# A third group of seven-product matrix forms in one gate stage, with one group's weight sums formed in SBUF

## The chip, the cores and the metric

The kernel runs on one core of one Trainium2 chip. The metric is the device time of one execution in microseconds (us); the time of a kernel is the median of its runs. Beside it one execution is profiled, and every duration below comes from that one. PE is the matrix engine (TensorE), DVE the vector engine, ACT the scalar engine, POOL is GpSimd, SP issues the plain loads.

## The reference, cut to what matters

Two layers work on 256 tokens of 1024 features in float32. Each layer is a feed-forward, a token mixer (causal pooling and attention, merged by gates) and a second feed-forward. Only the feed-forwards matter here:

```python
def swiglu(h, w_gate_up, w_down):
    a, b = jnp.split(h @ w_gate_up, 2, axis=-1)
    return (jax.nn.silu(a) * b) @ w_down

x = x + 0.5 * swiglu(rms_norm(x, ffn1_norm), ffn1_w_gate_up, ffn1_w_down)
...                                   # the token mixer
x = x + 0.5 * swiglu(rms_norm(x, ffn2_norm), ffn2_w_gate_up, ffn2_w_down)
```

`w_gate_up` has 2 x 2816 columns, 22 blocks of 128 for the gate and 22 for the other half. The results must stay float32-exact to a tight bound, so plain low-precision products are not enough.

## The kernel before, in words

**Units.** All weights lie in HBM as units of 128 x 2048 float32 (1 MB). A unit is loaded by SP into one of four `raw` buffers and split into two parts: ACT writes `hi`, the value rounded to the matrix engine's fast format (L209, two halves of 1024 columns), and DVE writes `lo` = raw - hi (L210). The activations are split in the same way. There are six half buffers each for hi and lo, so three units are split ahead of PE at most, and a split half waits until PE has read the half three units earlier.

**Pairs.** One unit of `w_gate_up` gives a gate block and its partner for all tokens: 16 products of a 512-column matmul (hi with both parts of x) and a 256-column one (lo with x's hi). The kernel calls that `pair`. The drained pair (ACT L258, DVE L259) is scaled, put through SiLU and multiplied in `post` (L465 to L474), and lands as two parts in a gate buffer: `ga`, `gb`, `gc` or `gd`.

**Groups and forms.** Four units can also be done as a group: x is cut into halves of its features and of its tokens, the weights likewise, and the 2 x 2 block product is made by seven products of sums of blocks instead of eight (Winograd's variant of Strassen). Each of the seven *forms* is half a unit's work for PE, but needs 1 MB of weights, loaded and split like a unit (L193 to L199). Forms 1, 2 and 3 read blocks of the weights as they lie; 4, 5, 6 and 7 read sums of blocks. Those sums are made long before, in DRAM: POOL copies one block to a DRAM tile and then lets the DMA add another (`go_on`, L183, one step a call, each behind the latest marked DVE result, L184). Form 6 starts from a copy of 7, form 4 from a copy of 6. `far_sums` lists the steps; the calls of `go_on` are spread over the whole kernel.

Products of a group accumulate in four PSUM banks, b0 to b3, each 128 x 512 (`banks4`). `seven` (L594) runs a form and combines its result: forms 1, 6 and 5 are copied out by ACT, forms 2, 5 and 4 are followed by a DVE addition that reads a bank (L607, L614, L619), and `gated` (L576 on ACT, L577 on DVE) multiplies SiLU of the gate half with its partner, for form 3 straight from the bank. The results have tokens on the partitions, so `turned` (t0, t1 of a group: four transposes each, L588) turns them through a bank, and ACT and DVE write the two parts from there to a gate buffer (L591, L592).

**Order.** PE's instructions keep the order of the program. The order of a gate stage is the tuple `TWO` or `THREE` (L54 to L57): a number is a pair, "7A" is form 7 of group A, "t1A" a turn, and (17, "t0B") a pair with a turn in its middle. The build orders the other engines' instructions itself; an engine takes them strictly in that order. The first feed-forward has no groups. The three others are called stage I (layer 0, second feed-forward, base `FU`, order TWO: 14 pairs, groups A and C), stage II (layer 1, first, base `LU`, order THREE: 10 pairs, groups A, B and C) and stage III (layer 1, second, THREE). In THREE, group B's products of forms 1, 6, 5, 3 go to b0 and those of A and C to b2; form 2 goes to b1, forms 7 and 4 to b3; t1 of A or B uses the bank of form 1, t0 uses b1, and C is turned during the down-projection that follows each gate stage.

Of the kernel before, what the change touches and what calls it, by code (L numbers as in the profile page):

```python
# [18 lines left out]
F32 = mybir.dt.float32  # L19
# [41 lines left out]
def groups_of(base):  # L61
    return "AC" if FEED[base] is TWO else "ABC"


def feed_units(base):

    for n in FEED[base]:
# [11 lines left out]
def trunk_kernel(ctx: ExitStack, tc: tile.TileContext, x_in, w_in, pw_in, qkn_in, rope_in, mask_in, band_in, out):  # L79
# [70 lines left out]
    far, steps_left = {}, []  # L150
# [9 lines left out]
    def far_sums():  # L160

        for base in STAGES:
            rest = []
            for g in groups_of(base):
# [21 lines left out]

    def sum_form(base, n):

        f, g = n
        z, hi, lo = buffers()  # L190
        src = quadrant(base, g, RAW[f]) if f in RAW else two_rows(far.pop((f, g, base)))
        z = two_rows(z)
        nc.sync.dma_start(z, src)  # L193
        z = z.rearrange("p i (k c) -> p i k c", c=2 * P)
# [5 lines left out]
        return hi, lo  # L200

    def buffers():
        raw = raws.tile([P, 2 * HALF], F32, name="raw", tag="raw")
        hi = [parts.tile([P, HALF], F32R, name="hi", tag="hi") for _ in range(2)]
        lo = [parts.tile([P, HALF], F32R, name="lo", tag="lo") for _ in range(2)]
        return raw, hi, lo
# [213 lines left out]
    def ffn(after, n0=0, end=False, col=None, base=0, far_at=(), steps_at=()):  # L420
        gs, gt = {}, {}

        def room(name, n0, m):
            g = acts.tile([P, m, 2, S], F32R, name=name, tag=name)
            gt[name] = g
            gs.update({n0 + i: g[:, i] for i in range(m)})

        def place(n):

            name, first = next(z for z in (("gb", 16), ("gd", 12), ("gc", 8), ("ga", 0)) if n >= z[1])  # L430
            return name, n - first

        room("ga", 0, 8)
        room("gc", 8, 4)
        room("gd", 12, 4)
        abs_, more = {}, []
        late_r = not (end and FEED[base] is TWO)
# [22 lines left out]
        def post(n):  # L460
# [10 lines left out]
            name, i = place(n)  # L471
            z = gt[name][:, i:i + 2]
# [4 lines left out]
        if n0:  # L477
            room("gb", 16, NF - 16)
# [17 lines left out]
        else:  # L496
# [12 lines left out]
            three = FEED[base] is THREE  # L509
            tk = {g: acts.tile([P, 2, GW], F32, name="tk", tag="tok", bufs=2) for g in ("AB" if three else "AC")}  # L510
            tk.setdefault("C", tk["A"])
# [13 lines left out]
            def x_forms():  # L525
# [26 lines left out]
                room("gb", 16, NF - 16)  # L552
# [27 lines left out]
            def turned(n, g):  # L580
# [3 lines left out]
                else:  # L584
                    pt = (bank["1" + g] if n == three else banks4[1]).rearrange("p (a s) -> p a s", s=S)
# [3 lines left out]
                name, i = place(GROUPS[g] + 2 * n)  # L589
                g = gt[name][:, i:i + 2]  # L590
# [3 lines left out]
            def seven(f, g):  # L594
# [3 lines left out]
                if f == "5":  # L598
                    if g == "B":
                        gated(p1, 0, 0, 0)  # L600
                    if three and g == "C":
                        p1 = tk["B"][:, 0]
                by_tokens(f, z, f in "127")
                if f == "1":
                    act(p1, z, AF.Copy)
                elif f == "2":
                    tt(p1, z, p1, op=OP.add)  # L607
                    if g != "B":
# [15 lines left out]
            if three:  # L624
                go_on()
# [532 lines left out]
```

## Time and profile before

| | |
|---|---|
| median of 3 runs | 994.12 us (994.01 to 995.92) |
| span of the profiled execution, first to last instruction | 991.9 us |
| PE busy | 986.1 us, 99% |
| DVE / ACT / POOL busy | 811.2 / 661.6 / 71.0 us |
| stage I, first gate matmul to first matmul of the down-projection | 325.38 to 439.74 |
| stage II | 499.37 to 612.01 |
| stage III | 815.18 to 927.82 |
| moved by DMA | 285.19 MB, mean 288 GB/s |
| loads of units and raw forms by SP (1 MB) | 168, median 7.2 us to landing |
| loads of sums by SP (1 MB) | 32, median 5.8 us to landing |
| steps in DRAM by POOL | 48 from the weights, 16 from another sum |

How to read the rows: a row of the groups has line, engine, operation, tiles (out<-in), shapes and count, then busy us and mean ns of one. A row of the timeline has start and duration in us, then the same names; "x2" marks two merged neighbours, and brackets hold the idle time before it and what ended it. Neighbours on DVE and ACT overlap a little. The ends of PE's matmuls are modelled, so the starts of its rows are what counts.

### The profile page before, as it was taken

Reading aid. Unit: us, or ns where it says so; the run is one execution under the profiler, and the core shown is the slowest. Engines: PE = TensorE matmul, PEld = TensorE weight load, DVE = VectorE, ACT = ScalarE, POOL = GpSimd, SP = SyncE. Lnnn points to the kernel's source line nnn. Section 1 sums busy time; section 2 is a strip of 40 time slices with the busy share of each in tenths; the row PEclk is TensorE's granted clock in tenths of the full one; section 3 lists DMA queues with packets and bytes.
Section 4 is the critical chain, followed back from the end, with each engine's and each line's share of the span. In section 5 each row is a group of like instructions: output and inputs, shape, how many; then the busy total and the mean of one; then the engine's idle time right before and its main releaser. Section 6 shows DMA issues by size and latency. Waiting matters only on the chain.

```text
span 991.9 us, 16162 instructions
## 1 busy us (share of the span) xinstructions
PE 986.1 (99%) x6296; PEld 895.4 (90%) x6296; DVE 811.2 (82%) x1154; ACT 661.6 (67%) x988; POOL 71.0 (7%) x111
## 2 busy tenths in 40 slices
PE   9999999999999999999999999999999999999998
PEld 8989888898899988889888889988988998888897
DVE  6987777698978798886779999776988887999872
ACT  7865555567766787775578877555677568887641
POOL 0000010104100000000000000000141000000000
PEclk9999999999999999999999999999999999999999
DMA  8889899989979769899979989898799998988840
GB/s 298 322 297 323 254 327 343 309 241 292 323 237 328 255 242 324 297 325 286 311 267 305 321 289 347 277 311 279 258 298 372 248 306 299 320 314 292 293 150 22
DMA packets 50269, 285.19 MB, mean 288 GB/s; under 512 B 4753, under 2 KB 6033, under 8 KB 27409
## 3 DMA queue, kind: packets, MB, share of 16 engines
q1 hardware_dynamic: 36624, 217.05, 58.8%
q0 software_dynamic: 13568, 67.11, 27.7%
q8 instruction: 49, 0.80, 0.3%
q14 instruction: 28, 0.22, 0.1%
HBM read 283.10 MB, written 68.16 MB: 354 GB/s over the span
## 4 chain that ended last, share of the span: by engine, by line
PE 99%; DMA 0%; DVE 0%; ACT 0%; SPq 0%; issue 0%
PE ps L110 68%; PE b L110 15%; PE pt L110 7%; PE two L110 4%; PE pe L110 1%; PE sc L110 1%; PE pt L780 1%; PE y L110 1%; PE b L588 0%; DMA raw<-w 0%; PE tp L736 0%; PE pt L588 0%; PE st L110 0%; PE ss L110 0%; DVE t L681 0%; ACT hi L209 0%
## 5 line engine op out<-in xcount | busy, mean ns | idle before, releaser
L210 DVE TENSOR_TENSOR lo<-raw,hi 128x1024 fp32r<-128x1024 f32 (+2 forms) x303 | 360.9, 1203 | 104.3 <-ACT hi L209 102.9
L209 ACT ACTIVATE hi<-raw 128x1024 fp32r<-128x1024 f32 (+2 forms) x303 | 310.6, 1033 | 194.8 <-PE ps L110 123.1
L110 PE MATMUL ps<-hx,hi 128*128 128x512 f32 x1184 | 400.2, 384 | 0.6 <-ACT hi L209 0.6
L110 PE MATMUL ps<-hx,lo 128*128 128x256 f32 x1184 | 323.7, 273 | 0.0
L110 PEld LDWEIGHTS ps<-hx,hi 128*128 128x128 f32 x1184 | 222.2, 188 | 40.7 <-ACT hi L209 0.8
L110 PEld LDWEIGHTS ps<-hx,lo 128*128 128x128 f32 x1184 | 222.5, 188 | 0.3 <-DVE lo L210 0.3
L199 DVE TENSOR_TENSOR lo<-raw,hi 128x1024 fp32r<-128x1024 f32 x112 | 135.0, 1220 | 17.7 <-ACT hi L198 17.5
L198 ACT ACTIVATE hi<-raw 128x1024 fp32r<-128x1024 f32 x112 | 117.5, 1056 | 41.4 <-PE ps L110 25.3
L110 PE MATMUL ps<-ga,hi 128*128 128x512 f32 (+1 forms) x264 | 87.8, 378 | 0.0
L110 PE MATMUL b<-hi,sf 128*128 128x512 f32 x256 | 87.4, 383 | 0.0
L183 POOL DMA_DIRECT2D f<-w x48 | 44.6, 932 | 557.7 <-DVE ab L259 239.4
L110 PE MATMUL b<-lo,sf 128*128 128x256 f32 x256 | 70.2, 274 | 0.0
L110 PE MATMUL ps<-ga,lo 128*128 128x256 f32 x256 | 69.9, 273 | 0.0
L110 PE MATMUL ps<-gb,hi 128*128 128x512 f32 (+1 forms) x198 | 65.4, 376 | 0.0
L110 PE MATMUL pt<-hi,hx 128*128 128x512 f32 x192 | 64.9, 384 | 0.0
L110 PE MATMUL b<-hi,hx 128*128 128x512 f32 x192 | 59.1, 388 | 0.0
L110 PEld LDWEIGHTS ps<-ga,hi 128*128 128x128 f32 x264 | 49.0, 188 | 8.2
L110 PEld LDWEIGHTS b<-hi,sf 128*128 128x128 f32 x256 | 48.0, 188 | 8.4
L110 PE MATMUL pt<-lo,hx 128*128 128x256 f32 x192 | 52.5, 274 | 0.0
L110 PE MATMUL ps<-gb,lo 128*128 128x256 f32 x192 | 52.4, 273 | 0.0
L110 PEld LDWEIGHTS ps<-ga,lo 128*128 128x128 f32 x256 | 48.1, 188 | 0.0
L110 PEld LDWEIGHTS b<-lo,sf 128*128 128x128 f32 x256 | 48.0, 188 | 0.0
(209 smaller groups left out, 1590.6 us busy)
## 6 DMA issues: line engine op xcount, KB each, us to landing
raw<-w SPq DMA_DIRECT2D x168, 1024.0 KB, 7.2
f<-w POOLq DMA_DIRECT2D x48, 1024.0 KB, 11.9
raw<-f SPq DMA_DIRECT2D x32, 1024.0 KB, 5.8
raw<-w SPq DMA_DIRECT2D x16, 256.0 KB, 5.3
out_dram<-gx SPq DMA_DIRECT2D x8, 128.0 KB, 1.9
gx<-x SPq DMA_DIRECT2D x3, 256.0 KB, 5.5
qk<-pw SPq DMA_DIRECT2D x2, 256.0 KB, 5.7
gx<-x SPq DMA_DIRECT2D x1, 300.0 KB, 2.8
```

The lines of the kernel that those rows point to most:

```text
L110: return keep(nc.tensor.matmul(*args, **kw))
L183: z = nc.gpsimd.dma_start(two_rows(far[f, g, base]), src, **kw)
L198: act(hv, a, AF.Copy)
L199: tt(lv, a, hv.bitcast(F32), op=OP.subtract)
L209: act(hi, w, AF.Copy)
L210: return tt(lo, w, hi.bitcast(F32), op=OP.subtract)
L780: keep(nc.tensor.transpose(pt[:, h, o * P:(o + 1) * P], pr[:, h, c * P:(c + 1) * P], ident))
```

## The change

- One order, `FEED`, with three groups now serves all three stages. Stage I so gets a group B: 10 pairs and 21 forms instead of 14 pairs and 14 forms. The forms stand in another order than in THREE, group C's spread over the stage.
- Group C's sums are no longer made in DRAM. `begin` loads a block by SP into a room in SBUF (the tiles of `gc` for 7, 6 and 4, of `gd` for 5), and POOL's DMA adds the second block there. Form 7C is split straight from the room; then POOL adds block 11 to the room for 6C, and after that split block 21 for 4C. The gate buffers `gc` and `gd` are allotted later for the results (`PLACES`), where the room is spent.
- The steps in DRAM fall from 64 to 48, with POOL's 12 additions into SBUF beside them; the calls of `go_on` are thinned.
- The banks: C has b0 (forms 1, 6, 5, 3) and b1 (7, 4); A and B have b2 (1, 6, 5, 3) and b3 (7, 4); form 2 of every group goes to b3. t1 of A or B turns through b2, t0 through b3.
- C's `gated(p1, 0, 0, 0)` moves from form 2 to form 3.

```diff
-TWO = (0, 1, "1A", 2, "2A", 3, 4, "7A", 5, "6A", 6, "5A", 7, "4A", "3A", 8, "t1A", "1C", (9, "t0A"), "2C", 10, "7C", 11, "6C",
-       16, "5C", 17, "4C", "3C")
-THREE = (0, 1, "1A", 2, "2A", "1B", 3, 4, "7A", "6A", 5, "5A", 6, "4A", "2B", "3A", "7B", "6B", 7, "t0A", "t1A", "5B",
-         16, "1C", "4B", "3B", "6C", (17, "t0B"), "7C", "t1B", "5C", "2C", "3C", "4C")
-FEED = {FU: TWO, LU: THREE, LU + FU: THREE}
+FEED = (0, 1, "+7C", "1A", "+5C", 2, "2A", "1C", 3, 4, "7A", "6A", 5, "5A", "7C", "4A", "3A", (6, "t1A"), "t0A", "1B", "2B", 7,
+        "6B", "7B", "5B", "6C", 16, "4B", "3B", "2C", "t1B", "5C", (17, "t0B"), "3C", "4C")
+PLACES = {"ga": range(8), "gb": (16, 17, 12, 13, 14, 15), "gd": range(8, 12), "gc": range(18, 22)}
+CHAIN = {"7": "11", "6": "21"}
...
+        while isinstance(u, tuple) and u[1][0] == "+":
+            begin(u[0], u[1][1:])
+            u = next(plan)
...
-            for g in groups_of(base):
+            for g in "AB":
...
+    def add_to(z, src):
+        nc.gpsimd.dma_start(two_rows(z), src, accum_op=OP.add)
+
+    def begin(base, n):
+        f, g = n
+        z = acts.tile([P, 2 * HALF], F32, name="c" + f, tag="gc" if f == "7" else "gd")
+        first, second = {"7": ("12", "22"), "5": ("11", "12")}[f]
+        nc.sync.dma_start(two_rows(z), quadrant(base, g, first))
+        add_to(z, quadrant(base, g, second))
+        near["5" if f == "5" else "764"] = z
+
     def sum_form(base, n):
         f, g = n
+        if g == "C" and f not in RAW:
+            hi, lo = halves_of_unit()
+            z = near["5" if f == "5" else "764"]
+            two_parts(z, hi, lo)
+            if f in CHAIN:
+                add_to(z, quadrant(base, g, CHAIN[f]))
+            return hi, lo
...
-            for g in groups_of(base):
-                for f in "1653":
-                    bank[f + g] = banks4[0 if (g == "B" if three else g == "A") else 2]
-                bank["2" + g] = banks4[1]
-                bank["7" + g] = banks4[3]
-                bank["4" + g] = banks4[3]
+            for g in GROUPS:
+                one, two = banks4[:2] if g == "C" else banks4[2:]
+                bank.update({f + g: one for f in "1653"})
+                bank.update({f + g: two for f in "74"})
+                bank["2" + g] = banks4[3]
...
-                    pt = (bank["1" + g] if n == three else banks4[1]).rearrange("p (a s) -> p a s", s=S)
+                    pt = bank["21"[n] + g].rearrange("p (a s) -> p a s", s=S)
...
-                name, i = place(GROUPS[g] + 2 * n)
-                g = gt[name][:, i:i + 2]
+                if GROUPS[g] not in gt:
+                    name = next(z for z in PLACES if GROUPS[g] in PLACES[z])
+                    room(name, PLACES[name])
+                g = gt[GROUPS[g] + 2 * n]
...
-            if l or h in (0, 2, 3, 4, 5, 7):
+            if h in (0, 2, 3, 4, 5, 7):
                 go_on()
...
-            far_at=(1,3,5,7,9) if l else (0,2,4,6,8,10), steps_at=(2,))
+            far_at=(1,3,5,7) if l else (0,2,4,6,8,10))
...
-            ffn(lambda f: prep(f, l + 1, C_G1), col=C_G2, base=FU, far_at=(1,3,5,7,9), steps_at=(3,6,10,16))
+            ffn(lambda f: prep(f, l + 1, C_G1), col=C_G2, base=FU, far_at=(1,5,9), steps_at=(3,))
```

How the new order moves instructions, at three places of stage II (stages I and III have the same order after the change). The line numbers of the changed kernel are its own.

First place: DVE, from the second lo half of the form ahead of 5A's addition. Before (`b3` is read by the additions of 5A, L614, and of 4A, L619; `vt` is what `gated` writes; `ab` belongs to the pairs):

```order
L199 TENSOR_TENSOR lo_5780<-raw_5776,hi_5778 128x2x2x256
L614 TENSOR_TENSOR tk_5313<-b3_5318,tk_5313 128x512
L465 TENSOR_TENSOR ab_5534<-ab_5534,r_5269 128x2x256
L199 TENSOR_TENSOR lo_5809<-raw_5806,hi_5807 128x2x2x256
L577 SCALAR_TENSOR_TENSOR vt_5312<-tk_5313,sg_5711 128x256
L470 TENSOR_TENSOR ab_5534<-ab_5534 128x2x256
L199 TENSOR_TENSOR lo_5810<-raw_5806,hi_5808 128x2x2x256
L259 TENSOR_TENSOR ab_5714<-ps_5715,ab_5714 128x512
L199 TENSOR_TENSOR lo_5836<-raw_5833,hi_5834 128x2x2x256
L619 TENSOR_TENSOR tk_5313<-b3_5318,tk_5313 128x512
```

And now (L634 and L639 are these additions, L595 is `gated`; the last row reads form 3A's bank b2):

```order
L221 TENSOR_TENSOR lo_5771<-raw_5767,hi_5769 128x2x2x256
L634 TENSOR_TENSOR tk_5321<-b3_5326,tk_5321 128x512
L233 TENSOR_TENSOR lo_5800<-raw_5797,hi_5798 128x1024
L233 TENSOR_TENSOR lo_5801<-raw_5797,hi_5799 128x1024
L595 SCALAR_TENSOR_TENSOR vt_5320<-tk_5321,sg_5722 128x256
L221 TENSOR_TENSOR lo_5855<-raw_5852,hi_5853 128x2x2x256
L639 TENSOR_TENSOR tk_5321<-b3_5326,tk_5321 128x512
L221 TENSOR_TENSOR lo_5856<-raw_5852,hi_5854 128x2x2x256
L221 TENSOR_TENSOR lo_5887<-raw_5884,hi_5885 128x2x2x256
L595 SCALAR_TENSOR_TENSOR vt_5320<-tk_5321,sg_5778 128x256
L221 TENSOR_TENSOR lo_5888<-raw_5884,hi_5886 128x2x2x256
L595 SCALAR_TENSOR_TENSOR vt_5320<-b2_5325,sg_5807 128x256
```

Behind 5A's addition now stand the splits of pair 6 and of forms 1B and 2B and three products of `gated`, with the additions; the scaling of a pair (L465, L470 before) has moved behind them. On PE, form 7C and not pair 6 stands between 5A and 4A.

Second place: DVE, around the turn t0A. Before, where t0A and t1A turn one after the other, through b1 and b2:

```order
L199 TENSOR_TENSOR lo_6035<-raw_6031,hi_6033 128x2x2x256
L259 TENSOR_TENSOR ab_5714<-ps_5899,ab_5714 128x512
L592 TENSOR_TENSOR gd_5192<-b1_5316,gd_5192 128x2x256
L592 TENSOR_TENSOR gd_5192<-b2_5317,gd_5192 128x2x256
L199 TENSOR_TENSOR lo_6060<-raw_6057,hi_6058 128x2x2x256
```

And now, where t0A turns through b3 behind pair 6:

```order
L233 TENSOR_TENSOR lo_5915<-raw_5911,hi_5913 128x1024
L282 TENSOR_TENSOR ab_5810<-ps_5811,ab_5810 128x512
L612 TENSOR_TENSOR gb_5545<-b3_5326,gb_5545 128x2x256
L221 TENSOR_TENSOR lo_5963<-raw_5960,hi_5961 128x2x2x256
L494 TENSOR_TENSOR ga_5200<-ab_5546,ga_5200 128x2x256
```

The reading of the turned bank stays behind the split and the drain; the bank is b3 now. On PE the turn is followed by form 1B on b2 and by form 2B on b3.

Third place: SP, around the start of stage II. Before:

```order
L193 DMA raw_5321<-w 128x2x1024
L143 DMA raw_5347<-w 128x2048
L193 DMA raw_5394<-w 128x2x1024
L193 DMA raw_5433<-w 128x2x1024
L143 DMA raw_5467<-w 128x2048
L143 DMA raw_5515<-w 128x2048
L193 DMA raw_5570<-f7_2096 128x2048
```

And now:

```order
L210 DMA raw_5331<-w 128x2x1024
L141 DMA raw_5360<-w 128x2048
L210 DMA raw_5407<-w 128x2x1024
L194 DMA c5_5357<-w 128x2x1024
L210 DMA raw_5445<-w 128x2x1024
L194 DMA c7_5328<-w 128x2x1024
L141 DMA raw_5479<-w 128x2048
L141 DMA raw_5527<-w 128x2048
L210 DMA raw_5582<-f7_2096 128x2048
```

The two room loads have come in, between the raw loads of 2A and 1C and behind that of 1C.

More of the change, by code (lines that the diff above doesn't have):

```diff
@@ L51 @@
 SUMS = (("7", "12", "22"), ("6", "7", "11"), ("5", "11", "12"), ("4", "6", "21"))
[L54 to L62 removed]
+FEED = (0, 1, "+7C", "1A", "+5C", 2, "2A", "1C", 3, 4, "7A", "6A", 5, "5A", "7C", "4A", "3A", (6, "t1A"), "t0A", "1B", "2B", 7,
+        "6B", "7B", "5B", "6C", 16, "4B", "3B", "2C", "t1B", "5C", (17, "t0B"), "3C", "4C")
+PLACES = {"ga": range(8), "gb": (16, 17, 12, 13, 14, 15), "gd": range(8, 12), "gc": range(18, 22)}
+CHAIN = {"7": "11", "6": "21"}
 def feed_units(base):
[L67 removed]
+    for n in FEED:
         n = n[0] if isinstance(n, tuple) else n
@@ L148, in fetch @@
         ahead.append((hi, lo))
-    far, steps_left = {}, []
+    far, steps_left, near = {}, [], {}
     def quadrant(base, g, q):
@@ L199, in sum_form, with halves_of_unit @@
             tt(lv, a, hv.bitcast(F32), op=OP.subtract)
-        return hi, lo
     def buffers():
-        raw = raws.tile([P, 2 * HALF], F32, name="raw", tag="raw")
+        return raws.tile([P, 2 * HALF], F32, name="raw", tag="raw"), *halves_of_unit()
+    def halves_of_unit():
         hi = [parts.tile([P, HALF], F32R, name="hi", tag="hi") for _ in range(2)]
         lo = [parts.tile([P, HALF], F32R, name="lo", tag="lo") for _ in range(2)]
-        return raw, hi, lo
+        return hi, lo
     def split(w, hi, lo):
@@ L421, in ffn, with room @@
         gs, gt = {}, {}
[L423 to L435, printed above, removed]
+        def room(name, ns):
+            g = acts.tile([P, len(ns), 2, S], F32R, name=name, tag=name)
+            for i, n in enumerate(ns):
+                gs[n] = g[:, i]
+                if i % 2 == 0:
+                    gt[n] = g[:, i:i + 2]
+        room("ga", PLACES["ga"])
+        if n0:
+            room("gc", range(8, 12))
+            room("gd", range(12, 16))
         abs_, more = {}, []
-        late_r = not (end and FEED[base] is TWO)
+        late_r = True
         last = {}
@@ L470, in post @@
             tt(g, g, u, op=OP.mult)
-            name, i = place(n)
-            z = gt[name][:, i:i + 2]
+            z = gt[n]
             act(z[:, :, 0, :], g, AF.Copy)
@@ L477, in ffn @@
         if n0:
-            room("gb", 16, NF - 16)
+            room("gb", range(16, NF))
             ws = [unit() for _ in range(n0)]
@@ L508, in ffn @@
             vt = acts.tile([P, 2, GW], F32, name="vt", tag="v")
-            three = FEED[base] is THREE
-            tk = {g: acts.tile([P, 2, GW], F32, name="tk", tag="tok", bufs=2) for g in ("AB" if three else "AC")}
-            tk.setdefault("C", tk["A"])
+            tk = {g: acts.tile([P, 2, GW], F32, name="tk", tag="tok", bufs=2) for g in "AC"}
+            tk["B"] = tk["A"]
             banks4 = [quarter(f"b{i}").rearrange("p a s -> p (a s)") for i in range(4)]
-            for g in groups_of(base):
-                for f in "1653":
-                    bank[f + g] = banks4[0 if (g == "B" if three else g == "A") else 2]
-                bank["2" + g] = banks4[1]
-                bank["7" + g] = banks4[3]
-                bank["4" + g] = banks4[3]
+            for g in GROUPS:
[3 more added lines that the diff above has]
+                bank["2" + g] = banks4[3]
             xg = pre[:, :NK * S].rearrange("p (k s) -> p k s", s=S)
@@ L551, in x_forms @@
                 parts_of("3", s4)
-                room("gb", 16, NF - 16)
+                room("gb", PLACES["gb"])
                 yield
@@ L598, in seven @@
                 if f == "5":
-                    if g == "B":
-                        gated(p1, 0, 0, 0)
-                    if three and g == "C":
+                    if g == "C":
                         p1 = tk["B"][:, 0]
+                if f + g == "3C":
+                    gated(p1, 0, 0, 0)
                 by_tokens(f, z, f in "127")
@@ L607, in seven @@
                     tt(p1, z, p1, op=OP.add)
-                    if g != "B":
+                    if g != "C":
                         gated(p1, 0, 0, 0)
@@ L623, in ffn @@
             xf = iter(())
-            if three:
-                go_on()
-            for n in FEED[base][2:]:
+            go_on()
+            for n in FEED[2:]:
+                if isinstance(n, str) and n[0] == "+":
+                    continue
                 next(xf, None)
@@ L637, in ffn @@
                     xf = x_forms()
-                    for _ in xf if not three else "":
-                        pass
                 if n % 2 and n > 1:
@@ L1064, in trunk_kernel @@
         if l + 1 < L:
-            ffn(lambda f: prep(f, l + 1, C_G1), col=C_G2, base=FU, far_at=(1,3,5,7,9), steps_at=(3,6,10,16))
+            ffn(lambda f: prep(f, l + 1, C_G1), col=C_G2, base=FU, far_at=(1,5,9), steps_at=(3,))
         else:
-            ffn(lambda f: nc.sync.dma_start(out[:, f, :], x[:, f, :]), end=True, col=C_G2, base=LU + FU, steps_at=(2,))
+            ffn(lambda f: nc.sync.dma_start(out[:, f, :], x[:, f, :]), end=True, col=C_G2, base=LU + FU)
 def _feat(a):
```

12 lines of the change are left out of this document (5 added, 7 removed).

## The prediction

> **What bounds the kernel now.** I read the page first, then the waits of the matrix engine (PE), then the three stages that the change touches.
>
> ```profile
> span 991.9 us, 16162 instructions
> PE 986.1 (99%) x6296; PEld 895.4 (90%) x6296; DVE 811.2 (82%) x1154; ACT 661.6 (67%) x988; POOL 71.0 (7%) x111
> PE busy L110 <- DVE eps L298: 1.1, 1, 1.1
> PE ps L110 <- ACT hi L209: 0.6, 1, 0.6
> ```
>
> The last two rows are all that PE waited for in the whole run (us in total, times, longest): both lie in the first 6 us. So the time is PE's own issue time. A change gains only by giving PE less to do, and every wait it brings PE is paid in full. The view by stretches of the three gate stages with matrix forms, each cut from its first gate matmul to the first matmul of its down-projection (the second row's ends follow it):
>
> ```profile
> core 0: us, PE busy (x) PEld busy (x) DVE busy (x) ACT busy (x) POOL busy (x), PEclk, DMA share, GB/s
> 325.38:439.74 114.36, 114.36 (x688) 102.61 (x687) 98.40 (x125) 85.74 (x116) 3.96 (x5) 1.00 0.83 289
> 499.37:612.01 112.64, 112.64 (x681) 101.13 (x679) 102.86 (x130) 92.19 (x124) 2.38 (x4) 1.00 0.87 305
> 815.18:927.82 112.64, 112.64 (x680) 101.12 (x679) 102.43 (x130) 92.24 (x125) 1.55 (x2) 1.00 0.86 307
> 325.38 0.39 PE L110 MATMUL ps<-hx,hi 128*128 128x512 f32 x1
> 439.74 0.39 PE L110 MATMUL ps<-ga,hi 128*128 128x512 f32 x1
> ```
>
> Stage I has two groups of forms, II and III three; I is 1.72 us longer. The clock column is 1.00. In II and III DVE is already 91% busy (102.86 of 112.64), so there the order of DVE's work decides whether PE finds a bank free.
>
> **The third group in stage I: a gain of 1.72 us.** Four pairs go, seven forms and eight transposes come.
>
> ```profile
> 347.68 10.68 PE ps L110 x64
> 548.34 0.38 PE L110 MATMUL ps<-hx,hi 128*128 128x512 f32 x1
> 545.66 0.38 PE L110 MATMUL b<-hi,sf 128*128 128x512 f32 x1
> 572.54 1.03 PE L588 MATMUL b<-ident,vt 128*128 128x128 f32 x8
> 573.34 0.47 PE L110 MATMUL b<-hi,sf 128*128 128x512 f32 x1
> ```
>
> Two pairs are 10.68, a pair 5.34; a form is 548.34 - 545.66 = 2.68 (from its first matmul to the next pair's); eight transposes 573.34 - 572.54 = 0.80. So 4 x 5.34 - 7 x 2.68 - 0.80 = 1.80. The two kinds of stage, run, differ by 1.72; I take that. DVE and ACT get as much to do in I as they have in II.
>
> **The new order and banks, in all three stages: three new waits.** Their order on DVE and ACT is the same in the three stages, so one is worked out, on the clock of stage II. Up to the end of 5A, PE has the same amounts in front of it as before (1C stands where 1B stood), so pair 5 ends at 545.66 again.
>
> First wait, 5A to 4A. Form 4A adds onto the bank of 7A (b3), and 5A's addition (L614, now L634) reads that bank. Before, pair 6 lay between 5A and 4A; now only form 7C. Natural start of 4A: 545.66 + 2 x 2.68 = 551.02. DVE's operations up to L634 are of the same kinds, in the same order and behind the same buffers as before's up to L614, so before's rows are its times:
>
> ```profile
> 545.80 1.06 ACT L198 ACTIVATE hi<-raw 128x1024 fp32r<-128x1024 f32 x1
> 546.90 1.23 DVE L199 TENSOR_TENSOR lo<-raw,hi 128x1024 fp32r<-128x1024 f32 x1
> 548.04 0.68 DVE L259 TENSOR_TENSOR ab<-ps,ab 128x512 f32<-128x512 f32 x1
> 548.64 2.35 DVE L199 TENSOR_TENSOR lo<-raw,hi 128x1024 fp32r<-128x1024 f32 x2
> 550.91 0.68 DVE L614 TENSOR_TENSOR tk<-b,tk 128x512 f32<-128x512 f32 x1
> 551.51 0.68 DVE L465 TENSOR_TENSOR ab<-ab,r 128x512 f32<-128x512 f32 x1
> ```
>
> The chain hangs on pair 5's end: ACT starts 0.14 behind it. The addition ends at 550.91 + 0.68 = 551.59. With 0.05 for the signal (an estimate, between the 0.03 and 0.14 that neighbouring rows here leave from end to start) 4A starts at 551.64: **0.62 late**.
>
> Second wait, 3A to t1A. The transposes t1A write the bank of 3A (b2), which 3A's product with the gate (L577, now L595) reads, and read that product. The gap is half a pair. Behind L634 the order puts ten operations on DVE, the last of which is that product: six lo halves, 4A's addition, three products. What each takes from start to next start:
>
> ```profile
> 559.54 0.42 DVE L577 SCALAR_TENSOR_TENSOR vt<-tk,sg 128x256 f32<-128x256 f32 x1
> 559.87 0.69 DVE L607 TENSOR_TENSOR tk<-b,tk 128x512 f32<-128x512 f32 x1
> 560.48 2.35 DVE L199 TENSOR_TENSOR lo<-raw,hi 128x1024 fp32r<-128x1024 f32 x2
> 562.74 1.22 DVE L210 TENSOR_TENSOR lo<-raw,hi 128x1024 fp32r<-128x1024 f32 x1
> ```
>
> A product 0.33, an addition 0.61, a lo half (562.74 - 560.48) / 2 = 1.13. From 551.51, where L634's successor starts: 6 x 1.13 + 0.61 + 2 x 0.33 = 8.05, so the product starts at 559.56 and ends at 559.98; PE may go at 560.03. ACT's halves end 0.1 us or more ahead of each lo half, those that wait for the late 4A too. PE, 0.62 late, is there at 545.66 + 4 x 2.68 + 2.67 + 0.62 = 559.67: **0.36 more**. Four forms in a row (5A, 7C, 4A, 3A) ask DVE for more than 2.68 each; before, a pair stood among them.
>
> Third wait, t0A to 2B. Both now use b3, with only 1B between; before, t0A went to b1, whose next user came much later. Before's own two turns show how long the emptying takes behind a pair that ends at 572.54:
>
> ```profile
> 572.68 1.06 ACT L198 ACTIVATE hi<-raw 128x1024 fp32r<-128x1024 f32 x1 [1.65 <-PE ps L110]
> 573.64 0.58 ACT L258 ACTIVATE ab<-ps 128x512 f32<-128x512 f32 x1
> 574.12 1.07 ACT L591 ACTIVATE gd<-b 128x512 fp32r<-128x512 f32 x2
> 573.77 1.23 DVE L199 TENSOR_TENSOR lo<-raw,hi 128x1024 fp32r<-128x1024 f32 x1 [0.28 <-ACT hi L198]
> 574.92 0.69 DVE L259 TENSOR_TENSOR ab<-ps,ab 128x512 f32<-128x512 f32 x1
> 575.52 1.28 DVE L592 TENSOR_TENSOR gd<-b,gd 128x512 fp32r<-128x512 f32 x2
> ```
>
> ACT splits a half, drains the pair, copies the bank; DVE follows with lo, drain, remainder. The first remainder starts 575.52 - 572.54 = 2.98 behind the pair and, with one addition's 0.68, ends at 3.66. The new order has these operations in this sequence behind pair 6. PE reaches 2B 0.40 (four transposes) + 2.68 = 3.08 behind the pair: 3.66 + 0.05 - 3.08 = **0.63 late**.
>
> Sum for a stage 0.62 + 0.36 + 0.63 = 1.61; three stages 4.83. PE works in order, so all behind a late matmul moves with it, and nothing behind has slack to give it back. The signal's price between 0 and 0.14 gives 1.5 to 1.8 a stage (the second wait gives back what the first takes, so their sum moves by one signal only).
>
> A rule against this change stands in the Trainium skill, VectorE: DVE Perf Modes, section "The DRAIN you can't avoid": the next operation starts only when the pipeline has emptied, unless it isn't held. If it always held, every lo half would cost its 1.22 and not 1.13, and the waits would grow by about 1 us a stage. The rows above disagree: successors start 0.08 to 0.09 before the end, so the sum stays with the rows.
>
> **Costed at nothing, with the cover.**
> - 4B to 2C (b3) and 3B to t1B (b2), by the same steps behind pair 16: lo, drain, lo, addition of 4B ends 1.23 + 1.15 + 0.60 + 1.13 + 0.68 = 4.79 behind the pair, 2C comes at 5.36; then lo, product, lo, product end at 7.72, t1B comes at 8.04. If DVE is 0.5 late there, t1B waits 0.2 a stage.
> - Room loads c5 and c7, ahead of raw loads on SP: in II the one waits for the last read of gd, the other for that of gc, the end of the down-projection before. Behind c7 stand pairs 3 and 4. Pair 3 is needed 3 x 5.34 + 3 x 2.68 = 24 us into the stage, and its raw buffer comes free only about when the stage starts, as before. Its load is the fourth of 1 MB in flight there, with two additions beside: 4 to 6 x 1.05 MB at some 300 GB/s (stretch rows) are 14 to 21 us, and a split half 2.3. Without this cover it costs what the load is late.
> - POOL's additions into SBUF. ACT's split of 6C waits for one and the queue behind it too. No addition into SBUF is in the trace; the nearest:
>
> ```profile
> f<-w POOLq DMA_DIRECT2D x48, 1024.0 KB, 11.9
> DMA to landing us min/median/max: 4.7/8.1/19.6
> ```
>
>  From 7C's split to 6C's lie over 30 us, from 6C's to 4C's over 20: bounds 0 and, if each took 19.6 behind another, a few us. I take 0. Four fewer POOL DMAs and 6 fewer raw loads free no PE time, since PE never waits for a load now.
> - The steps moved out of the gate stages and the mixers go on an idle POOL (71.0 of 991.9 us), each with tens of us till its use.
>
> **Sum:** 991.9 - 1.72 + 4.83 = 995.0 for the profiled execution; the median of the runs lies 2.2 above the span, so 994.12 + 3.11 = **997.2**.
>
> **Rivals.**
> 1. The gain alone: DVE and ACT are ahead of my chain by a us, and no bank is late. For it: no PE wait in 990 us. Against: before never puts a bank's reader and its next writer one form apart there. 994.12 - 1.72 = 992.4.
> 2. One kind of wait only (the chain of forms or t0A, not both): 3 x 0.6 to 3 x 1.0 against 1.72, 994.2 to 995.5. For it: the two hang on different chains. Against: both are worked from rows of this very place.
> 3. Slower than mine: loads or additions land later among the denser forms, or the 0.3 left at t1B goes too. Each further us of DVE lag costs 3: with 1 us a stage 1000.2. It decides from the point at which a landing comes after the split's turn on ACT. For it: DMA share already 0.87 in II. Against: fewer bytes in II and III. With lo halves at their full 1.22 it would come out here too, at 997.2 + 3 x 1.0 = 1000.2. (That is the first half of the section named above from the Trainium skill, VectorE: DVE Perf Modes.)
>
> **Numbers.** Mine 0.60 (own range 995.9 to 998.8), rival 1 0.14, rival 2 0.14, rival 3 0.12. About 0.2% (2.0 us) is what a measurement can tell from no change: faster means under 992.1, slower over 996.1. Rival 1 lies just inside, so faster gets 0.07; same 0.26 (rest of 1, all of 2, the low edge of mine); slower 0.67. The range 993.2 to 999.3 leaves out most of 1 and of 3.
>
> **What would show it.** Stage lengths near 114.2 in all three, instead of 114.36, 112.64, 112.64. In the waits of PE three rows of about 0.6, 0.4 and 0.6 in each stage, ended by DVE at the addition of 5A (L634), the product of 3A (L595) and the remainder of t0A (L612). Stages of 112.6 prove the waits wrong; PE waits ended by ACT's split or a DMA prove my zeros wrong; a stage I that isn't like II proves the gain wrong.

## The result, and the profile after

The changed kernel takes 1007.37 us (median of 4 runs, 1005.44 to 1008.37), the kernel before 994.30 beside it: 1.0124 times as long, 95% interval 1.0109 to 1.0140. Forecast were 997.2 us and a range of 993.2 to 999.3. The direction is right and the size is not: 13 us were lost, 3 were forecast.

From the page of the changed kernel: span, PE's busy time and the shares of the chain that ended last; then all rows of the waits of PE that this change could have brought (us in total, times, longest).

```profile
span 1005.7 us, 16162 instructions
PE 989.4 (98%) x6288; PEld 896.3 (89%) x6288; DVE 816.2 (81%) x1159; ACT 668.7 (66%) x995; POOL 71.7 (7%) x107
PE 89%; DVE 4%; DMA 4%; ACT 2%; issue 1%; SPq 0%; ACTq 0%; DVEq 0%
PE b L606 <- DVE vt L595: 6.1, 3, 4.5
PE b L105 <- DVE tk L634: 3.9, 3, 1.8
PE b L105 <- DVE gb L612: 1.0, 3, 0.4
```

The three rows are the forecast ones, one in each stage: 5A's addition (L634), 3A's product (L595), t0A's remainder (L612). They were expected at 1.9, 1.1 and 1.9 us in all. The third is smaller, the first is twice as large, the second nearly six times. The 4% DMA in the chain are new; before, it was

```profile
PE 99%; DMA 0%; DVE 0%; ACT 0%; SPq 0%; issue 0%
```

A wait that DVE ends can hang on a load that landed late. The three stages, by stretches (us, then busy us and count of PE, PEld, DVE, ACT, POOL, then granted clock, DMA share, GB/s):

```profile
325.62:447.96 122.34, 115.92 (x680) 103.23 (x679) 103.43 (x130) 92.60 (x124) 5.02 (x5) 0.97 0.84 274
507.53:623.57 116.04, 113.56 (x680) 101.23 (x679) 103.76 (x130) 92.41 (x125) 6.67 (x7) 1.00 0.91 300
826.52:941.92 115.40, 113.37 (x680) 101.20 (x679) 103.33 (x130) 92.71 (x124) 2.37 (x2) 1.00 0.79 272
```

All three do the same work (680 matmuls) in the same order, and before, II and III took 112.65 and 112.64 us. Now they differ by up to 7 us, stage I is the longest and its clock is 0.97. An order alone can't do that, since it is the same order. The chain of waits through the longest wait, in stage I (start, us, what; pieces under 0.1 us left out):

```profile
367.76 17.05 DMA raw<-w
...
384.92 1.07 ACT hi L220
386.01 1.23 DVE lo L221
387.23 0.20 DVE tk L639
387.44 0.32 issue
387.75 1.24 DVE lo L221 x2
388.99 1.03 issue
390.02 0.31 DVE vt L595
390.35 1.22 DVE lo L221
391.57 0.34 DVE vt L595
391.96 1.11 PE b L606 x4
```

The load of form 1B took 17.05 us. ACT and DVE work in program order; 1B's split and 2B's stand ahead of 3A's product, which needed neither. So the product (391.57) and with it t1A (391.96) waited for data that PE wants only later: 1B's behind the rest of pair 6 and t0A, 2B's behind 1B.

### The profile page after: what moved, and what is told of

It reads as the page before. It is cut to its first block, busy times and chain, and to the rows that moved or that the text cites. A ratio compares the mean times of both kernels' runs of the same rounds, so it can differ in the third digit from the quotient of the medians.

```text
span 1005.7 us, 16162 instructions
## 1 busy us (share of the span) xinstructions
PE 989.4 (98%) x6288; PEld 896.3 (89%) x6288; DVE 816.2 (81%) x1159; ACT 668.7 (66%) x995; POOL 71.7 (7%) x107
## 4 chain that ended last, share of the span: by engine, by line
PE 89%; DVE 4%; DMA 4%; ACT 2%; issue 1%; SPq 0%; ACTq 0%; DVEq 0%
PE ps L105 62%; PE b L105 12%; PE pt L105 7%; PE two L105 4%; DMA raw<-w 4%; DVE lo L221 2%; PE pe L105 1%; PE sc L105 1%; DVE lo L233 1%; ACT hi L232 1%; ACT hi L220 1%; PE pt L799 1%; PE y L105 1%; PE b L606 1%; DVE ab L282 0%
## 5 line engine op out<-in xcount | busy, mean ns | idle before, releaser
L233 DVE TENSOR_TENSOR lo<-raw,hi 128x1024 fp32r<-128x1024 f32 (+2 forms) x295 | 350.9, 1199 | 112.5 <-ACT hi L232 111.0
L105 PE MATMUL ps<-hx,hi 128*128 128x512 f32 x1120 | 381.0, 386 | 0.5 <-ACT hi L232 0.5
L105 PE MATMUL ps<-hx,lo 128*128 128x256 f32 x1120 | 307.2, 274 | 0.0
L105 PEld LDWEIGHTS ps<-hx,hi 128*128 128x128 f32 x1120 | 211.3, 189 | 38.6 <-ACT hi L232 0.7
L105 PEld LDWEIGHTS ps<-hx,lo 128*128 128x128 f32 x1120 | 211.5, 189 | 0.3 <-DVE lo L233 0.3
L221 DVE TENSOR_TENSOR lo<-raw,hi 128x1024 fp32r<-128x1024 f32 x102 | 122.4, 1217 | 20.5 <-ACT hi L220 18.9
L220 ACT ACTIVATE hi<-raw 128x1024 fp32r<-128x1024 f32 x102 | 106.5, 1055 | 34.9 <-PE ps L105 18.9
L105 PE MATMUL b<-hi,sf 128*128 128x512 f32 x288 | 97.9, 383 | 0.0
L105 PE MATMUL b<-lo,sf 128*128 128x256 f32 x288 | 79.0, 274 | 0.0
L181 POOL DMA_DIRECT2D f<-w x36 | 33.5, 931 | 424.1 <-DVE ab L282 152.0
```

The lines of the kernel that those rows point to most:

```text
L105: return keep(nc.tensor.matmul(*args, **kw))
L181: z = nc.gpsimd.dma_start(two_rows(far[f, g, base]), src, **kw)
L220: act(hv, a, AF.Copy)
L221: tt(lv, a, hv.bitcast(F32), op=OP.subtract)
L233: return tt(lo, w, hi.bitcast(F32), op=OP.subtract)
```

## The experiments

Theory O: the order and the banks make the waits, about 1.6 us a stage, even when every load is in time. Theory M: the transfers that the change puts beside the weight loads (POOL's additions into the rooms, and the step in DRAM that `steps_at=(3,)` issues inside stage I) make loads late. They are told apart by taking away the transfers, the order, or both. One more step stands early in stage I (issued at 340.69 us in the change) and one early in stage II (522.94 us); of the runs below only those of experiments 1, 2 and 4 take these away.

Stage lengths below are cut as above, each from one profiled execution. Where no load is late they repeat within 0.02 us (the kernel before and experiment 2). With the additions they do not: stage III took 115.40 us in the change and 114.27 in the kernel of experiment 5 that alters nothing in that stage. So a difference of about a us between two such stages is not resolved.

### 1. No transfer of POOL's, the order kept

```diff
 def go_on():
-    if not steps_left:
-        return
+    return
 def add_to(z, src):
-    nc.gpsimd.dma_start(two_rows(z), src, accum_op=OP.add)
+    return
...
-    src = quadrant(base, g, RAW[f]) if f in RAW else two_rows(far.pop((f, g, base)))
+    src = quadrant(base, g, RAW[f] if f in RAW else {"7": "12", "6": "11", "5": "11", "4": "21"}[f])
```

A form of sums so reads its first block from the weights, and its other blocks are left out.

> The changed kernel without any of GpSimd's transfers: each form that is a sum of blocks reads its first block alone, so that part of the computation is left out; orders of forms, banks, splits, groups and the early room loads stay. Theory O (order and banks: a product of one form keeps a bank that the next but one needs, and the VectorE chain sets the time): the three waits stay at about 1.6 us in each stage and the time is about 997.2 us, as forecast. Theory M (memory: the added transfers make the weight loads land late, and the late loads make the waits): no wait of VectorE's that is over 0.2 us is left in the three stages and the time is about 992.4 us. If both have a part, the waits fall to the forecast 1.6 us a stage, those of 4.67 us and 1.9 us vanish, and it is 997 us.

Measured: 997.48 us (7 runs), ratio 1.0033, interval 1.0022 to 1.0044. Waits of PE, then the stages by stretches:

```profile
PE b L105 <- DVE tk L633: 1.7, 3, 0.8
PE b L105 <- DVE gb L611: 1.1, 3, 0.4
325.75:440.25 114.50, 113.56 (x680) 101.25 (x679) 103.29 (x130) 92.75 (x124) 0.00 (x0) 1.00 0.70 244
499.81:614.17 114.36, 113.52 (x681) 101.22 (x679) 103.65 (x130) 93.13 (x125) 0.15 (x1) 1.00 0.76 258
817.12:931.67 114.55, 113.34 (x681) 101.18 (x679) 103.28 (x130) 92.65 (x124) 0.00 (x0) 1.00 0.70 244
```

(Its line numbers are one lower.) The stages are alike again, and at 114.4 to 114.6 us where the prediction's sum gave 112.64 + 1.61 = 114.25. With loads in time the forecast time is what comes out, in part by luck: the gain was smaller than forecast and so were the waits, and the two errors partly cancel (below). The other 10.4 us of the three stages (10.3 of the spans, 1005.7 and 995.4; 9.9 of the medians) come and go with POOL's transfers.

### 2. The same for the kernel before

```diff
 def go_on():
-    if not steps_left:
-        return
+    return
...
-    src = quadrant(base, g, RAW[f]) if f in RAW else two_rows(far.pop((f, g, base)))
+    src = quadrant(base, g, RAW[f] if f in RAW else {"7": "12", "6": "11", "5": "11", "4": "21"}[f])
```

> A control: the kernel before without any of GpSimd's transfers (each sum of blocks reads its first block alone: part of the computation is left out). Theory O: its loads were in time already, 994.0 to 994.4 us. Theory M says the same as long as the transfers of the kernel before slow nothing; if they cost it too, 992 to 993.5 us, and the other two kernels without transfers are then to be compared with this one.

Measured: 994.23 us (10 runs), ratio 1.0002, interval 0.9992 to 1.0011. The kernel before had 64 steps in DRAM and lost nothing by them that shows. So experiment 1 can be compared with it as it is.

### 3. Another order, all transfers kept

```diff
-FEED = (..., 5, "5A", "7C", "4A", "3A", (6, "t1A"), "t0A", "1B", "2B", 7,
-        "6B", "7B", "5B", "6C", 16, "4B", "3B", "2C", "t1B", "5C", (17, "t0B"), "3C", "4C")
+FEED = (..., 5, "5A", 6, "4A", "3A", "7C", (7, "t1A"), "t0A", "1B", 16, "2B",
+        "6B", "6C", "7B", "5B", 17, "4B", "3B", "2C", "t1B", "5C", "t0B", "3C", "4C")
```

> The changed kernel with all its transfers, its forms' table alone changed: a pair stands between 5A and 4A, 7C and a pair between 3A and t1A, a pair between 1B and 2B, so that every one of the three waits has 3 us or more of other matmuls ahead. Theory O: the three waits vanish and the time is the gain alone, about 992.5 us. Theory M: late loads hold up whatever form comes next; the waits move and the time stays at 1004 to 1008 us. Both: the 1.6 us a stage are saved, 1001 to 1003 us.

Measured: 1001.46 us (4 runs), ratio 1.0066, interval 1.0049 to 1.0082. Waits of PE, then the stages:

```profile
PE b L105 <- ACT tk L633: 3.2, 3, 1.1
PE b L105 <- DVE tk L634: 2.2, 2, 1.9
327.61:446.20 118.59, 115.27 (x680) 102.51 (x679) 102.67 (x129) 91.54 (x124) 5.02 (x5) 0.99 0.88 289
505.76:620.11 114.35, 113.27 (x681) 101.18 (x680) 103.03 (x129) 92.33 (x125) 6.68 (x7) 1.00 0.94 310
823.06:937.43 114.37, 113.29 (x680) 101.24 (x679) 102.86 (x129) 92.27 (x124) 2.37 (x2) 1.00 0.79 272
```

The three old waits are gone from II and III, although all additions are still there. But the table made a new one of its own, 1.1 us in each stage: pair 17 had stood between 5C and 3C, which share b0; with it moved away, 3C waits for ACT's copy of 5C (L633). In stage I the late loads still cost 4.2 us more than in II, now through L634 and a clock of 0.99.

### 4. That order without POOL's transfers

Experiments 1 and 3 together.

> The table with pairs between and without any of GpSimd's transfers (each sum of blocks reads its first block alone: part of the computation is left out). Both theories: neither waits nor late loads, so what is left is the gain of the third group in the first of the stages: about 992.4 us; the three stages take 112.3 to 113.2 us each. Over 993.5 us: the gain of 1.72 us was mis-sized, or there is a third cause.

Measured: 997.39 us (7 runs), ratio 1.0032, interval 1.0021 to 1.0043; all three stages 114.35 to 114.37 us, and of PE's waits in them only one row is left (L632 is L633 of the change):

```profile
PE b L105 <- ACT tk L632: 3.2, 3, 1.1
```

The expected 992.4 us missed by 5.0. Most of that is this wait, 3 x 1.24 us: the three old waits were traded for one of nearly their sum. The run gives the base, though. By the starts of its neighbours on PE, less the usual pitch, the wait is 1.24 us a stage, so 113.1 are left, where 112.64 was forecast: the rest of the miss.

### 5. The additions left out, the step kept; and the reverse

```diff
 def add_to(z, src):
-    nc.gpsimd.dma_start(two_rows(z), src, accum_op=OP.add)
+    return
```

> The changed kernel with the additions into the rooms left out (six of GpSimd's transfers a stage fewer or so; the third group's sums read their first block alone, so that part of the computation is left out); the DRAM steps all stay, the one inside the first of the three stages too. The stages took 122.34, 116.04 and 115.40 us with everything, 114.50, 114.36 and 114.55 us with no transfer of GpSimd's. If the additions into the rooms make the loads late: the second and third stage fall to 114.4 and 114.6 us, the first keeps at most 1 us from the step, 998 to 999 us. If the DRAM step does it: the first stays over 119 us and it is 1003 to 1006 us.

```diff
-    ffn(..., base=FU, far_at=(1,5,9), steps_at=(3,))
+    ffn(..., base=FU, far_at=(1,3,5,9))
```

> The changed kernel with one DRAM step moved from pair 3 of the first of the three stages to its second matrix, where weight loads are in hand; nothing left out. If that step (issued beside a room's addition, landing after 14 us) is what made the first stage lose its 4.67 us and the clock: that stage falls from 122.34 to 115 to 116.5 us, the others stay, 1000 to 1002 us. If the additions into the rooms do it: 121 to 122.5 us and 1006 to 1008 us.

(There are four additions a stage, twelve in all; the "six" in the first expectation is a slip.) Measured: 998.60 us without the additions (3 runs, ratio 1.0041, interval 1.0025 to 1.0057), 1000.09 without the step in stage I (2 runs, ratio 1.0056, interval 1.0036 to 1.0077). Stages I and II, first without the additions, then without the step:

```profile
326.03:441.39 115.36, 113.40 (x681) 101.20 (x680) 103.33 (x130) 92.74 (x124) 2.60 (x3) 1.00 0.77 261
500.94:615.35 114.41, 113.58 (x681) 101.25 (x680) 103.62 (x130) 93.13 (x125) 1.89 (x3) 1.00 0.77 268
```

```profile
325.51:440.62 115.11, 113.39 (x680) 101.21 (x679) 103.25 (x130) 92.83 (x124) 4.46 (x4) 1.00 0.85 282
500.18:616.18 116.00, 113.47 (x680) 101.19 (x679) 103.71 (x130) 92.31 (x125) 6.69 (x7) 1.00 0.91 299
```

Both expectations for stage I came true, which their wording took to exclude each other. Over the 114.50 us with neither, the step without additions costs stage I 0.86, the additions without that step 0.61, both together 7.84. The two small costs are no larger than the scatter named above; the sum of both is far beyond it, and the medians of the runs say the same (998.60 and 1000.09 against 1007.37). (Stage III fell from 115.40 to 114.27 us without the step, which stands in another stage; why stays open.) Stage II costs 1.6 us more with the additions than without them, in the change as in the run without the step of stage I. Its own early step is there in both and costs nothing that shows without additions (114.41 against 114.36); additions without it were not run.

The landing times say why. DMA issues (out<-in, engine, count, KB, median us to landing) in the 35 us of stage I around the wait (from 357 on), of the change, without the additions, and without the step:

```profile
raw<-w SPq DMA_DIRECT2D x5, 1024.0 KB, 12.9
f<-w POOLq DMA_DIRECT2D x1, 1024.0 KB, 13.8
c<-w POOLq DMA_DIRECT2D x1, 1024.0 KB, 13.3
```

```profile
raw<-w SPq DMA_DIRECT2D x5, 1024.0 KB, 11.7
```

```profile
raw<-w SPq DMA_DIRECT2D x5, 1024.0 KB, 7.8
```

In experiment 1 the same row says 5.3, of nine loads, because the sums too come from the weights there; the five loads of the other rows took 5.0 to 6.9 us. The medians don't follow the costs (11.7 us goes with 0.86, 7.8 with 0.61, 12.9 with 7.84). One load does: that of 1B, issued at 367.6 to 368.2 us of each run. It took 6.9 us with neither, 7.8 without the step, 12.1 without the additions and 17.05 with both. ACT's first split of 1B, in the same order of runs from the second on:

```profile
379.30 1.06 ACT L220 ACTIVATE hi<-raw 128x1024 fp32r<-128x1024 f32 x1 [0.55 <-ACT sg L594]
380.87 1.06 ACT L220 ACTIVATE hi<-raw 128x1024 fp32r<-128x1024 f32 x1 [0.69 <-PE b L105]
384.92 2.01 ACT L220 ACTIVATE hi<-raw 128x1024 fp32r<-128x1024 f32 x2 [3.94 <-DMA raw<-w]
```

A load has from its issue, when a raw buffer is free, to its turn on ACT; here that is about 13 us. At 12.1 us 1B is in time by 0.6 us, and ACT waits for PE to free a half buffer; at 17.05 it is 3.94 us late. That is how two causes of under a us each can make a large one. (The 0.86 and 0.61 come by other loads: 3A's took 12.1 us without the additions and holds up 5A's addition, a wait of 1.5 us; 2B's took 8.6 us without the step and holds up 3A's product, a wait of 0.9 us.)

The clock adds to it. Around the end of the wait of 4.5 us the granted clock falls to a half. By stretches of 5 us, the change:

```profile
387.00:392.00 5.00, 0.48 (x4) 0.19 (x3) 5.00 (x8) 3.71 (x5) 0.00 (x0) 0.84 0.97 380
392.00:397.00 5.00, 5.00 (x17) 4.42 (x18) 2.93 (x4) 1.12 (x2) 0.00 (x0) 0.50 0.77 320
```

PE is busy for 115.92 us in stage I and for 113.56 in II with the same matmuls: 2.4 of the 7.84 us are the clock.

### 6. The additions as plain copies

```diff
 def add_to(z, src):
-    nc.gpsimd.dma_start(two_rows(z), src, accum_op=OP.add)
+    nc.gpsimd.dma_start(two_rows(z), src)
```

> The changed kernel, its additions into the rooms issued from the same queue, at the same places and of the same blocks, but as plain copies, so that the sums of the third group are wrong parts of the computation; the DRAM step stands inside the first stage. If it is the number of transfers and their bytes that make the loads late: the first stage stays at 119 to 122.5 us and it is 1004 to 1008 us. If it is that they add (they land after 13.5 us in the median, the plain loads of the same rooms after 7.5): 115 to 116 us in the first and 114.4 in the second stage, 998 to 1000 us.

Measured: 1000.84 us (2 runs), ratio 1.0067, interval 1.0047 to 1.0087. Stages I and II, then ACT's first split of 1B:

```profile
325.68:444.74 119.06, 115.04 (x680) 102.50 (x679) 103.37 (x130) 92.59 (x124) 4.12 (x5) 0.99 0.79 270
504.30:618.70 114.40, 113.47 (x681) 101.28 (x680) 103.55 (x130) 92.89 (x125) 4.78 (x7) 1.00 0.85 304
382.64 2.01 ACT L220 ACTIVATE hi<-raw 128x1024 fp32r<-128x1024 f32 x2 [1.92 <-DMA raw<-w]
```

The answer lies between. In stage II the whole excess goes (114.40, as with no transfer of POOL's at all): there it is the adding. In stage I 3.3 of 7.84 us go, and the other 4.6 stay with the same number of transfers of the same size. The load of 1B took 14.7 us, and ACT waited 1.92 us for it: between the 12.1 us that were still in time and the 17.05 that came 3.94 us late.

### 7. The rooms loaded later

```diff
-FEED = (0, 1, "+7C", "1A", "+5C", 2, "2A", "1C", 3, 4, "7A", ..., (6, "t1A"), "t0A", "1B", "2B", 7,
+FEED = (0, 1, "1A", 2, "2A", "1C", 3, 4, "+7C", "7A", ..., (6, "t1A"), "t0A", "1B", "+5C", "2B", 7,
-    ffn(..., base=FU, far_at=(1,5,9), steps_at=(3,))
+    ffn(..., base=FU, far_at=(1,3,5,9))
```

> The changed kernel's own order of forms, but the two rooms loaded later (the one behind pair 4, the other behind 1B, where the change has them ahead of 1A and of 2A), and the DRAM step out of the first stage; nothing is left out. With the step out and the rooms early the stages took 115.11, 116.00 and 114.27 us. If the pile of room loads, additions and one step at the start of the second stage makes its loads late: the second falls to 114.4 us, with the first wait at 0.64 us, 998.3 us. If the additions do it wherever they stand: 115.5 to 117 us, their cost moves into the run of forms, 999.5 to 1002 us.

Measured: 1002.05 us (2 runs), ratio 1.0077, interval 1.0052 to 1.0103; stages 115.64, 115.76 and 114.95 us, against 115.11, 116.00 and 114.27 with the rooms early. The medians, of two runs each, do not tell the two apart (1002.05 us with runs of 1000.26 and 1003.83; 1000.09 with 998.97 and 1001.20).

The run doesn't test what it was made for, because the transfers hardly moved. In stage II the first addition is issued 3.7 us behind the stage's start, where it was 3.5 with the rooms early, and the second 17.5 us where it was 11.1:

```profile
504.69 1.22 POOL L187 DMA_DIRECT2D c<-w  x1 [15.08 <-DMA c<-w]
518.55 1.19 POOL L187 DMA_DIRECT2D c<-w  x1 [12.64 <-PE ps L105]
```

The table says where a room is loaded in the program; the build orders SP's loads itself, and the first stayed at the front. PE's waits in stage II changed places: 0.7 instead of 1.8 us at 5A's addition (L634), 1.0 instead of 0.4 at 3A's product (L595). Whether the pile of transfers at the start of stage II makes its 1.6 us stays open.

### 8. An order with cover for every bank

First try: table 3 with 5C ahead of t1B, and 2C, 3C, t0B, 4C behind, with and without the step in stage I.

```diff
-..., 17, "4B", "3B", "2C", "t1B", "5C", "t0B", "3C", "4C")
+..., 17, "4B", "3B", "5C", "t1B", "2C", "3C", "t0B", "4C")
```

> The table with pairs between, its end mended: 5C ahead of t1B, then 2C, 3C, t0B, 4C, so that 5C's bank has 2C behind it and the wait of 1.24 us in front of 3C goes. All transfers as in the changed kernel, nothing left out. The second and third stage took 114.35 us with that wait and no late load: they should take 113.1 us; the first keeps what its late loads cost (118.6 less 1.24 us, 117.4 us). Order and late loads both, each in its place: 997.5 us. If late loads come back in the second and third stage: over 1000 us.

> The same mended table and the DRAM step moved out of the first stage into its second matrix; nothing left out. If step and late loads are one cause, all three stages take 113.1 to 113.5 us: 994.3 less 1.25 us of the first and plus 0.46 in each of the others, 993.6 to 994.5 us. If the additions into the rooms are enough to make the loads late: the first stage stays over 116 us and it is 996 us or more.

Measured: 1021.64 and 1017.31 us (4 runs each), ratios 1.0271 and 1.0232 (intervals 1.0256 to 1.0287, 1.0215 to 1.0249). The table was wrong in a way that the expectations overlooked: the tile `vt` holds the products that a turn reads. 5C writes one of them before t1B has read group B's, and 3C one before t0B has. So part of the computation changes (group B's turned products are partly C's), and each turn now waits for the form just ahead of it. These runs tell nothing on theories O and M. They show the price of a dependence that the table's author forgot: PE's wait row of the first run is

```profile
PE b L606 <- DVE vt L595: 15.2, 6, 3.9
```

Second try, the turns in their old order, and the step out of stage I (the table replaces the change's):

```diff
+FEED = (0, 1, "+7C", "1A", "+5C", 2, "2A", 3, 4, "7A", "6A", 5, "5A", 6, "4A", "3A", "7C", (7, "t1A"), "t0A", "1B", "1C", "2B",
+        "6B", "7B", "5B", "6C", 16, "4B", "3B", (17, "t0B"), "t1B", "5C", "2C", "3C", "4C")
-    ffn(..., base=FU, far_at=(1,5,9), steps_at=(3,))
+    ffn(..., base=FU, far_at=(1,3,5,9))
```

> A table with cover for all of the waits and the turns in their old order (the table before it put 5C ahead of t1B, whose products then stood in the place of the turn's): pair 6 between 5A and 4A, 7C and half of pair 7 between 3A and t1A, 1C between 1B and 2B, 6C and pair 16 between 5B and 4B, 2C between 5C and 3C; the DRAM step is moved out of the first stage; nothing is left out. Theory O with loads in time: no wait of over 0.2 us, 112.7 to 113.1 us a stage, 993 to 993.8 us. If the additions into the rooms still make loads late where no form can wait for them: the second stage stays at 114.5 us or more, 995 to 996 us.

Measured: 993.26 us (10 runs), ratio 0.9985, interval 0.9975 to 0.9994: faster than the change, and 0.15% faster than the kernel before by an interval that just leaves out 1. In the three stages PE waits for nothing:

```profile
325.40:438.37 112.97, 112.97 (x681) 101.22 (x680) 101.96 (x129) 92.22 (x124) 4.47 (x4) 1.00 0.88 290
497.99:611.02 113.03, 113.03 (x680) 101.22 (x679) 102.33 (x129) 92.43 (x125) 6.67 (x7) 1.00 0.94 313
813.98:926.94 112.96, 112.96 (x681) 101.22 (x679) 101.97 (x129) 92.22 (x124) 2.37 (x2) 1.00 0.80 275
```

Stage II has a DMA share of 0.94, over the change's 0.91, and the same additions that cost the change's order 1.6 us. They are free here, as they were in stages II and III of experiment 3: by the new table a pair or another form lies between each reader of a bank and its next writer, which a late split can use up.

And with the step back in stage I (`far_at=(1,5,9), steps_at=(3,)`):

> The last table (1C between 1B and 2B and so on, 993.26 us with the DRAM step moved) with the step back inside the first of the three stages; nothing is left out. If the covers of the order hide what late loads cost: stages of 113 us as before, 993.0 to 994.0 us. If step and additions together make loads late there and no order hides it: the first stage takes 116 to 119 us (it took 118.59 with another table that had covers), 996 to 1000 us, with the wait in front of a form whose split is late.

Measured: 994.97 us (10 runs), ratio 1.0003, interval 0.9993 to 1.0013.

```profile
327.73:441.88 114.15, 113.42 (x680) 101.22 (x679) 101.94 (x129) 92.06 (x124) 5.02 (x5) 1.00 0.90 299
```

That is 1.18 us for step and additions together (over the 112.97 without the step), where the change's order pays 7.84. Between the two expectations: the covers take most of what late loads cost, not all.

## Why the prediction was wrong, point by point

| us | before | forecast | no waits (8) | order's waits, loads in time (1) | the change |
|---|---|---|---|---|---|
| stage I | 114.36 | 114.25 | 112.97 | 114.50 | 122.34 |
| stage II | 112.65 | 114.25 | 113.03 | 114.36 | 116.04 |
| stage III | 112.64 | 114.25 | 112.96 | 114.55 | 115.40 |
| sum | 339.65 | 342.75 | 338.96 | 343.41 | 353.78 |

- **What bounds it** (PE's own time, every wait paid in full): right. The stages' sum grew by 14.1 us, the span by 13.8.
- **The gain, 1.72 us:** right in kind, too large. Stage I fell by 1.39 us with no wait in it, and II and III grew by 0.38 and 0.32, so the sum gained 0.69. The growth isn't one wait; it is spread over the pitch of the 512-column matmuls (in stage III from start to start, before and in experiment 8: 222.7 and 224.1 ns in pairs, 225.1 and 225.8 in forms). What sets this pitch wasn't tried, and experiment 8 has another table than the change.
- **Three waits, 1.61 us a stage:** right in place, releaser and size as long as loads are in time. Experiment 1 less experiment 8 is 1.53, 1.33 and 1.59 us, 4.45 in all against 4.83. One by one (starts of the neighbours on PE, less the usual pitch): 0.64 to 0.91 for the first, forecast 0.62; 0.23 for the second, forecast 0.36; 0.46 to 0.54 for the third, forecast 0.63. Reading DVE's old rows forward through the new order worked to a few tenths. The rule weighed there, the Trainium skill's on "The DRAIN you can't avoid" (VectorE: DVE Perf Modes), would have made each stage about 1 us longer; no stage of experiment 1 was.
- **4B to 2C and 3B to t1B at nothing:** right, no wait at either.
- **Room loads and POOL's additions at nothing: the step that failed.** "I take 0" was worth 10.4 us together with the steps (experiment 1). Without the additions alone the stages fall from 353.78 to 344.31 us, without the step of stage I alone to 345.38 (experiment 5). The prediction argued its margin for the room loads against pair 3 alone, and for the additions by what waits for *them*, the next form of group C. No wait of ACT for a room stands in the trace. What the additions do is slow the plain loads beside them: 1B's from 6.9 us to 17.05 with step and addition, where the order leaves about 13. A bound was in the prediction (a landing of 19.6 us was quoted), but it was carried to the additions and not to the raw loads. Its sign of wrong zeros, PE waits ended by ACT's split or a DMA, didn't show either: the late split stood on DVE ahead of the product that PE waited for, so DVE ended the wait.
- **"The steps moved ... go on an idle POOL":** true of POOL, beside the point. The step left inside stage I was never costed as a transfer, since the kernel before had steps there as well; it lost nothing by them (experiment 2).
- **The third rival** (loads land late among the denser forms, 1000.2 us, 0.12) had the mechanism and the point from which it decides. It looked to the denser forms and not to POOL's transfers, and it was priced at the same 1 us in every stage. Lateness isn't so even: it is free up to the margin, under a us in stage I for each cause alone, 7.8 for both, of which the clock made 2.4, which no case had.

Seen whole: -0.69 + 4.45 + 10.37 = 14.13 us by the table; forecast -1.72 + 4.83 + 0 = 3.11.

## What to carry to other kernels

When an order is made denser, price the transfers beside it by how much later the *other* loads land and compare that with the slack of every split standing ahead of work that PE needs at once; "nobody waits for this transfer" is not a price. Two causes that eat one margin must be tried together, since each alone can look free. Look in the trace whether an edit moved the transfers that it was to move (experiment 7's hardly did). And where two forms share a bank, put something between them before counting the gain: the same third group, with each bank covered and one step moved, turned a loss of 1.24% into a gain of 0.15% (an interval of 0.06 to 0.25%).

## What the runs showed of the hardware that was not expected

- **Additions into SBUF were dear for their neighbours.** In the first 22.5 us of stage II the change moved 320 GB/s and POOL's two additions landed after 16.3 us (median); as plain copies of the same blocks, 376 GB/s and 11.0 us, with the 16 DMA engines nearly full in both. The Trainium skill says in DMA: Bandwidth & Descriptors, section "Issuing engines are not separate DMA queues", that transfers of all engines interleave on the same 16 DMA engines. The trace agrees: five loads of SP in stage I took 5.0 to 6.9 us without POOL's transfers (experiment 1) and 11.4 to 17.0 with them (the change).
- **The clock fell after shorter waits than one might think, and not after each longer one.** Waits of up to 1.95 us left it at 1.00 (stage II of the change and of experiment 5). One of 2.07 us (experiment 3, stage I, no other wait of PE ahead of it in the stage) and one of 2.26 (experiment 6, stage I) were followed by matmuls at half speed for 3.4 us, the wait of 4.5 us in the change for 6.8. In these two experiments the stage's average was 0.99, PE busy 115.27 and 115.04 us instead of 113.3 to 113.5. In the broken table of experiment 8 waits of 3.8 to 4.0 us brought every stage of the first run to 0.97, but one of 2.18 us there (stage I) left the clock at 1.00, and so did one of 3.8 us in stage II of the second run. The Trainium skill, TensorE: Matmul & The Clock Gate, Part 1, gives about 3.4 us of idleness for the fall to a half. The half is what the trace shows (0.50); the shortest wait behind which it fell was 2.07 us. The length of the wait alone doesn't decide it, so this is no threshold.
